# Down-projection as seven streamed products instead of full products in six groups of inner tiles

## The chip, the cores and the metric

One core of a Trainium2 chip runs the kernel. The metric is the device time of one execution in microseconds (us). TensorE (PE) multiplies, VectorE (DVE), ScalarE (ACT) and GpSimd (POOL) do the elementwise work, and SyncE (SP) issues most transfers. Each engine works its own queue in order; semaphores hold an instruction until what it needs is there.

## The reference

One layer for 1024 tokens of width 1024, in fp32: a token mixer and its output projection, a layer norm over a scaled residual, a gated MLP with a causal convolution, and a second layer norm. The change lies in the last product of the MLP.

```python
def layer_norm(x, g, b):
    ...
    y = (xf - mu) * lax.rsqrt(var + LN_EPS)
    return (y * g + b).astype(x.dtype)

def conv_gated_mlp(h, w_up, conv_w, conv_b, w_down):
    u = jnp.einsum('btd,df->btf', h, w_up)
    ...
    uc = conv_b + sum(conv_w[j] * up[:, j:j + T] for j in range(CONV_WIDTH))
    a, v = jnp.split(uc, 2, axis=-1)
    return jnp.einsum('btf,fd->btd', jax.nn.gelu(a) * v, w_down)
    ...
    h = layer_norm(ALPHA * h + mix, ln1_g[l], ln1_b[l])
    ffn = conv_gated_mlp(h, w_up[l], conv_w[l], conv_b[l], w_down[l])
    h = layer_norm(ALPHA * h + ffn, ln2_g[l], ln2_b[l])
```

T = 1024 tokens, D = 1024, 2816 inner channels, which are 22 tiles of 128 (`f` = 0 to 21).

## The kernel before

**Products.** An fp32 operand is split into a high part (`split`, L69, a copy to fp32r on ACT) and a low part (L70, a subtraction on DVE). `mm3` (L86 to L89) makes a product of three matmuls: high by high, high by low, low by high. One matmul has a 128x128 stationary tile and 512 columns. A `unit` is a PSUM tile of 128x1024, two banks.

**Up-projection.** It is a form of Strassen's scheme already. `prep(f)` loads the two weight tiles of f and makes seven combinations on DVE; `pair(f)` runs seven products, 84 matmuls, and puts them together in `ua` and `uv` (L688, L691, L694 on DVE); `post(f)` is the convolution of both (L698 on ACT, L700 on DVE), the GELU (L710, ACT), the product of the gate (L712, DVE) and one store of the gated tile to DRAM, `gd[f]` (L713, 512 KB). They are generators; `step` runs the pieces of pair(f), post(f-1) and prep(f+1) in turn, and this order, with the tile scheduler's, sets the queues.

**Down-projection.** The 22 inner tiles come in groups of 2, 4, 4, 4, 4, 4 (`GRP`). For a group, each of the 8 token tiles t and both column halves are multiplied over the inner tiles of the group in PSUM: 22 x 8 x 2 x 3 = 1056 matmuls. DVE then adds the unit to `z[t]` in SBUF (L811 in the first group, with the shift of the residual; L813 in the others). For the next group, `down_weight(f)` and `gated(f)` load a tile of w_down and one of `gd` through SP into `raw` (three buffers) and split them: weights into `wh`/`wl` or `dh`/`dl`, gated tiles into the eight places of `bh` and `bl`. `residual()` loads `zn` from `zd[t]` (L788) and adds it, scaled, to z[t] (L789, L790 on DVE).

**Layer norm.** In the last group z[t] is drained (L801), its statistics are taken (L500, L471), `rs` is made on GpSimd (L463, L464), and z is scaled. Tiles 1, 3, 5 and 6 do it "spread": L476 on DVE, L477 on ACT, the addition of beta on GpSimd (L480), a store through SP (L481). The others use two operations on DVE (L491, L495) and L497; the last tile in halves.

Of the kernel before, what the change touches and what calls it, by code (L numbers as in the profile page):

```python
# [27 lines left out]
GRP = (2,) + (4,) * 5  # L28
# [9 lines left out]
SPLIT = 5  # L38
SPREAD = (1, 3, 5, 6)
# [6 lines left out]
def block_kernel(ctx: ExitStack, tc: tile.TileContext, x, xT, w_ct, w_i, pool_w, w_out, w_up, w_down, pk, rows, masks, ident, out):  # L46
# [7 lines left out]
    big = ctx.enter_context(tc.tile_pool(name="big", bufs=1))  # L54
# [646 lines left out]

    def post(f):
        a, v = outs.pop(f)
        cv, ca = (ug.tile([P, T], F32, tag=f"c{n}", name=f"c{n}") for n in "va")
# [8 lines left out]
        nc.sync.dma_start(out=gd[f], in_=ca)  # L713
# [49 lines left out]
    def first_group():
        for f in groups[0]:
            down_weight(f)
            yield
        for i in range(3):
            yield
        for f in groups[0]:
            gated(f)  # L770
            yield
# [118 lines left out]
```

## Time and profile before

| | us |
|---|---|
| median of three runs | 1072.68 (1071.88 to 1073.37) |
| the profiled execution | 1071.9 |
| its span | 1070.0 |
| PE busy | 1055.3 (99%), 4812 matmuls |
| DVE busy | 767.2 (72%) |
| ACT busy | 402.6 (38%) |
| GpSimd busy | 50.9 (5%) |
| end of the up-projection's last matmul | 820.4 |
| end of the last matmul | 1060.8 |

Busy time is counted per engine; matmuls are pipelined, so the distance from start to start is the cost of one. A number in square brackets behind a row is the time that the engine was idle before it, with the operation that released it.

### The profile page before, as it was taken

To read this page: it belongs to the slowest core of one execution; us is meant where nothing else is said; L and a number is where in the kernel's file an instruction comes from. 1 tells how busy PE (TensorE), PEld (TensorE's weight loads), DVE (VectorE), ACT (ScalarE), POOL (GpSimd) and SP (SyncE) were. 2 spreads that over 40 slices of the span, in tenths; PEclk is the share of its full clock that TensorE was granted. 3 is DMA by queue.
4 is the path that set the end of the run, shared out by engine and by line. 5 is a ranking of instruction groups with operands and counts; after the bars stand their busy time and mean duration, and the time that the engine had idled before them with its cause. 6 is when DMAs were issued, how large, how long until landed. Compare 5 with 4: busy or idle time off the path is not lost.

```text
span 1070.0 us, 11956 instructions
## 1 busy us (share of the span) xinstructions
PE 1055.3 (99%) x4812; PEld 861.5 (81%) x4812; DVE 767.2 (72%) x891; ACT 402.6 (38%) x500; POOL 50.9 (5%) x71
## 2 busy tenths in 40 slices
PE   8999999999999999999999999999999999999996
PEld 6888888888888877887777778778777888888885
DVE  6585498877736689877868868778778965634178
ACT  5422453223713474544434444445355312202001
POOL 2000000011000100000000000000000000000035
PEclk9999999999999999999999999999999999999999
DMA  8200211100142313231231221322326644321012
GB/s 319 90 20 1 79 40 40 40 1 20 41 177 99 122 75 118 79 118 60 72 106 59 89 89 59 112 65 62 116 79 216 236 138 157 119 97 59 1 60 99
DMA packets 27848, 97.13 MB, mean 91 GB/s; under 512 B 3088, under 2 KB 3984, under 8 KB 27792
## 3 DMA queue, kind: packets, MB, share of 16 engines
q1 hardware_dynamic: 27648, 96.29, 26.3%
q8 instruction: 38, 0.62, 0.2%
q14 instruction: 18, 0.15, 0.0%
q10 hardware_dynamic: 144, 0.07, 0.0%
HBM read 76.42 MB, written 19.92 MB: 90 GB/s over the span
## 4 chain that ended last, share of the span: by engine, by line
PE 89%; DVE 4%; POOL 2%; ACT 2%; DMA 2%; issue 1%; SPq 0%; POOLq 0%; DVEq 0%; ACTq 0%
PE u L87 28%; PE u L89 28%; PE u L88 28%; PE u L230 3%; POOL rs L463 1%; POOL z L480 1%; PE u L270 1%; PE u L272 1%; PE u L259 1%; DMA hg<-in_xT 1%; ACT hq L533 1%; DVE st L500 1%; DVE wl L70 1%; DMA raw<-gd 0%; DVE bl L70 0%
## 5 line engine op out<-in xcount | busy, mean ns | idle before, releaser
L87 PE MATMUL u<-bh,wh 128*128 128x512 f32 x520 | 206.2, 398 | 2.9 <-DVE uv L691 1.3
L88 PE MATMUL u<-bl,wh 128*128 128x512 f32 x520 | 203.0, 390 | 1.0 <-DVE bl L70 1.0
L89 PE MATMUL u<-bh,wl 128*128 128x512 f32 x520 | 203.0, 391 | 0.0
L69 ACT ACTIVATE wh<-raw 128x1024 fp32r<-128x1024 f32 x97 | 100.7, 1058 | 133.2 <-PE u L88 100.8
L70 DVE TENSOR_TENSOR wl<-raw,wh 128x1024 fp32r<-128x1024 f32 x97 | 116.8, 1223 | 28.1 <-ACT wh L69 25.7
L87 PE MATMUL u<-wh,bh 128*128 128x512 f32 x336 | 132.6, 395 | 0.0
L89 PE MATMUL u<-wh,bl 128*128 128x512 f32 x336 | 131.1, 390 | 0.0
L88 PE MATMUL u<-wl,bh 128*128 128x512 f32 x336 | 131.0, 390 | 0.0
L87 PEld LDWEIGHTS u<-bh,wh 128*128 128x128 f32 x520 | 97.7, 188 | 30.3 <-DVE uv L691 7.7
L88 PEld LDWEIGHTS u<-bl,wh 128*128 128x128 f32 x520 | 97.7, 188 | 20.8 <-DVE bl L70 1.6
L89 PEld LDWEIGHTS u<-bh,wl 128*128 128x128 f32 x520 | 97.6, 188 | 20.7
L87 PE MATMUL u<-th,wh 128*128 128x512 f32 x264 | 105.5, 400 | 0.0
L89 PE MATMUL u<-th,wl 128*128 128x512 f32 x264 | 103.6, 393 | 0.5 <-DVE wl L70 0.5
L88 PE MATMUL u<-tlo,wh 128*128 128x512 f32 x264 | 103.1, 391 | 0.0
L813 DVE TENSOR_TENSOR z<-u,z 128x1024 f32<-128x1024 f32 x32 | 39.1, 1223 | 62.2 <-PE u L89 62.2
L89 PEld LDWEIGHTS u<-wh,bl 128*128 128x128 f32 x336 | 63.1, 188 | 13.5
L88 PEld LDWEIGHTS u<-wl,bh 128*128 128x128 f32 x336 | 63.2, 188 | 13.1
L87 PEld LDWEIGHTS u<-wh,bh 128*128 128x128 f32 x336 | 63.1, 188 | 13.1
L87 PEld LDWEIGHTS u<-th,wh 128*128 128x128 f32 x264 | 49.5, 187 | 18.4 <-DVE uv L688 4.3
L88 PE MATMUL u<-dl,bh 128*128 128x512 f32 x160 | 63.4, 396 | 0.0
L89 PE MATMUL u<-dh,bl 128*128 128x512 f32 x160 | 63.4, 396 | 0.0
L87 PE MATMUL u<-dh,bh 128*128 128x512 f32 x160 | 63.3, 396 | 0.0
(175 smaller groups left out, 1631.8 us busy)
## 6 DMA issues: line engine op xcount, KB each, us to landing
raw<-in_w_up SPq DMA_DIRECT2D x42, 512.0 KB, 3.4
gd<-ca SPq DMA_DIRECT2D x22, 512.0 KB, 5.3
raw<-in_w_down SPq DMA_DIRECT2D x22, 512.0 KB, 4.3
raw<-gd SPq DMA_DIRECT2D x22, 512.0 KB, 4.0
raw<-in_w_ct SPq DMA_DIRECT2D x13, 512.0 KB, 3.3
raw<-in_w_out SPq DMA_DIRECT2D x8, 512.0 KB, 3.2
z<-in_x SPq DMA_DIRECT2D x8, 512.0 KB, 4.1
zd<-z SPq DMA_DIRECT2D x8, 512.0 KB, 2.6
```

Source lines behind the costliest of these rows:

```text
L69: A.activation(out=h, in_=r, func=AF.Copy)
L70: V.tensor_tensor(out=l, in0=r, in1=h.bitcast(F32), op=ALU.subtract)
L87: PE.matmul(o, lhsT=ah, rhs=bh, start=start, stop=False, **kw)
L88: PE.matmul(o, lhsT=ah, rhs=bl, start=False, stop=False, **kw)
L89: PE.matmul(o, lhsT=al, rhs=bh, start=False, stop=stop, **kw)
L230: PE.matmul(ul[:, p * P:(p + 1) * P], lhsT=km[:, p * P:(p + 1) * P], rhs=view(QF, p * P + hh, [2 * hh, 64 // hh], [512 - hh, 2], [1, hh]), ...
L259: PE.matmul(up[:, c * P:(c + 1) * P], lhsT=KTr[:, c * P:(c + 1) * P], rhs=vchunk(c, hs), start=True, stop=True)
L270: PE.matmul(uo[:, cs], lhsT=vchunk(c, hs), rhs=sc[:, cs], start=True, stop=c == 0)
L272: PE.matmul(uo[:, cs], lhsT=S[:, (c - 1) * P:c * P], rhs=QF[:, cs], start=False, stop=True)
L463: G.tensor_scalar(out=rs, in0=mv[:, 1:2], scalar1=LN_EPS, scalar2=None, op0=ALU.add)
L480: G.tensor_tensor(out=zt[:, c], in0=zt[:, c], in1=bet[:, c], op=ALU.add)
L813: V.tensor_tensor(out=z[t], in0=u, in1=z[t], op=ALU.add)
```

## The change

**Products.** The down-projection becomes seven products of halves: token halves (`lo`, `hi` of 512), even and odd inner tiles, column halves. Each has 11 pairs of inner tiles, 4 token tiles and 512 columns: 7 x 11 x 4 x 3 = 924 matmuls. They run as seven rounds over all inner channels in the order P1, P2, P6, P5, P7, P3, P4. A round has six steps (`jps`): five of two pairs, 24 matmuls, and one of a single pair, 12.

**PSUM.** A round's four token tiles keep four banks for the whole inner sum. P1, P6, P7 and P4 use one set, P2, P5 and P3 the other; P6, P7 and P3 go on from the sum that stands there. `finish` (L877, L880) adds a bank to z once per round.

**Gated side.** `post` stores seven kinds of 128x512 blocks (`gd["11"]` to `gd["s4"]`) per pair of f, 2 KB to a row, and makes the four combinations on DVE (L718, L720, L723, L725). For each step SP loads the two blocks (`load_a`, L769).

**Weights.** Blocks of w_down are loaded by 24 transfers through GpSimd's queue (`load_w2`, L852) into `ww`, in memory that the up-projection's operands held; only two for P1 go through SP into `rawb` (L797). Combinations are made on DVE in `prepare` (L806, L811, L818, L820), and each operand is split one step ahead (L65 on ACT, L66 on DVE).

**Layer norm.** Tiles 0 to 5 are "added": L472 on DVE, L473 on ACT, then a transfer from GpSimd's queue that adds the row of beta to z (L474), then the store (L475). Tile 6 is "whole", tile 7 in halves on DVE. In P4 token tiles 0 and 1 run together through all steps, then 2, then 3.

```diff
-GRP = (2,) + (4,) * 5
...
+    jps = [(j, j + 1) if j + 1 < NF // 2 else (j,) for j in range(0, NF // 2, 2)]
+    gd = {(n, i): tc.dram_tile([P, len(js), 512], F32, name=f"gd{n}{i}")
+          for n in ("11", "12", "22", "s1", "s2", "s3", "s4") for i, js in enumerate(jps)}
...
-        if how == "spread":
+        if how == "added":
             V.scalar_tensor_tensor(out=zt, in0=zt, scalar=mv[:, 0:1], in1=gam, op0=ALU.subtract, op1=ALU.mult)
             A.activation(out=zt, in_=zt, func=AF.Identity, scale=rs)
-            def shift(c):
-                G.tensor_tensor(out=zt[:, c], in0=zt[:, c], in1=bet[:, c], op=ALU.add)
-                nc.sync.dma_start(out=sink[:, c], in_=zt[:, c])
-            if last:
-                shift(halves[0])
-                late_shift.append(lambda: shift(halves[1]))
-            else:
-                shift(whole)
+            G.dma_start(out=zt, in_=rows[3:4, :].broadcast_to([P, D]), accum_op=ALU.add)
+            nc.sync.dma_start(out=sink, in_=zt)
...
+    def store(n, j, src):
+        nc.sync.dma_start(out=gd[n, j // 2][:, j % 2, :], in_=src)
...
-        nc.sync.dma_start(out=gd[f], in_=ca)
+        j = f // 2
+        if f % 2 == 0:
+            gated[j] = ca
+            store("11", j, ca[:, lo])
+            return
+        store("12", j, ca[:, lo])
+        store("22", j, ca[:, hi])
+        yield
+        g1 = gated.pop(j)
+        sm = ug.tile([P, T], F32, tag="cv", name="sm")
+        V.tensor_tensor(out=sm[:, lo], in0=g1[:, lo], in1=g1[:, hi], op=ALU.add)
+        store("s3", j, sm[:, lo])
+        V.tensor_tensor(out=g1[:, hi], in0=g1[:, hi], in1=ca[:, hi], op=ALU.add)
+        store("s1", j, g1[:, hi])
+        yield
+        V.tensor_tensor(out=sm[:, hi], in0=g1[:, hi], in1=g1[:, lo], op=ALU.add)
+        store("s2", j, sm[:, hi])
+        V.tensor_tensor(out=g1[:, lo], in0=sm[:, hi], in1=ca[:, lo], op=ALU.add)
+        store("s4", j, g1[:, lo])
...
-    wd = [None] * NF
-    def down_weight(f):
-        if f % 10 < 5:
-            wd[f] = weight(w_down[f])
-            return
-        r = raw(w_down[f])
-        wd[f] = [dn.tile([P, 1024], F32R, tag=f"d{n}", name=f"d{n}") for n in "hl"]
-        split(r, *wd[f])
-    def gated(f):
-        r = raw(gd[f])
-        split(r, bh[:, f % 8, :], bl[:, f % 8, :])
...
+    order = ("11", "12", "s2", "s1", "s3", "s4", "22")
+    P1, P2, P6, P5, P7, P3, P4 = range(7)
+    plan = [(i, q) for i in range(7) for q in range(NS)]
+    raw_a, opsd = {}, {}
+    def load_a(n):
+        i, q = plan[n]
+        r = raw_a[n] = rawp.tile([P, 2, 512], F32, tag="raw", name="rawa")
+        nc.sync.dma_start(out=r[:, :len(jps[q]), :], in_=gd[order[i], q])
...
+    def slot(n):
+        if n >= 2 * NS * P4 and n - 2 * NS * P4 < 4:
+            t = zq.tile([P, 4, 512], F32R, tag=f"w0{n - 2 * NS * P4}", name="p4")
+            return t[:, 0:2], t[:, 2:4]
+        if n % 8 < 5:
+            return [t.rearrange("p (a t) -> p a t", t=512) for t in wpair()]
+        return [dn.tile([P, 2, 512], F32R, tag=f"d{e}", name=f"d{e}") for e in "hl"]
...
+    def prepare(n):
+        i, q = plan[n]
+        k = len(jps[q])
+        a = split2(raw_a.pop(n)[:, :k, :], 2 * n, k)
+        if i == P1 and q < 2:
+            src = rawp.tile([P, 2, 512], F32, tag="raw", name="rawb")[:, :k]
+            nc.sync.dma_start(out=src, in_=w_view(0, q, lo))
+        elif i == P1:
+            src = w_block(0, q, lo)
+        elif i == P2:
+            src = w_block(1, q, lo)
+            w11 = w_block(0, q, lo)
+        elif i == P6:
+            w21, w22 = w_block(1, q, lo), w_block(1, q, hi)
+            src = zq.tile([P, 2, 512], F32, tag="t2", name="t2")[:, :k]
+            V.scalar_tensor_tensor(out=src, in0=w_block(0, q, lo), scalar=-1.0, in1=w22, op0=ALU.mult, op1=ALU.subtract)
+        elif i == P5:
+            src = w_block(0, q, lo)
+        elif i == P7:
+            src = w_block(0, q, hi)
+            V.tensor_tensor(out=src, in0=w_block(1, q, hi), in1=src, op=ALU.subtract)
+        elif i == P3:
+            src = w_block(1, q, hi)
+        else:
+            src = w_block(1, q, lo)
+        opsd[n] = a, split2(src, 2 * n + 1, k)
+        if i == P2:
+            V.tensor_tensor(out=w11, in0=w11, in1=w_block(0, q, hi), op=ALU.subtract)
+        elif i == P6:
+            V.tensor_tensor(out=w21, in0=w21, in1=src, op=ALU.add)
...
+    step([pair(NF - 1), post(NF - 2), first_operands()], 7)
+    last_post = post(NF - 1)
+    step([last_post], 7)
...
+    w_loads = [(0, q, lo) for q in range(2, NS)] + [(1, q, lo) for q in range(NS)] + [(0, q, lo) for q in range(2)] + \
+              [(0, q, hi) for q in range(NS)] + [(1, q, hi) for q in range(NS)]
+    def load_w2(n):
+        for r_, q, c in w_loads[:n]:
+            G.dma_start(out=w_block(r_, q, c), in_=w_view(r_, q, c))
+        del w_loads[:n]
...
-            for u, c in zip(us, halves):
-                for f in fs:
-                    mm3(u[:, c], bh[:, f % 8, ts], bl[:, f % 8, ts], wd[f][0][:, c], wd[f][1][:, c], f == fs[0], f == fs[-1])
-                if last and t >= SPLIT:
-                    drain(u, c)
-            if not last:
-                if gi == 0:
-                    V.scalar_tensor_tensor(out=z[t], in0=b1_, scalar=ALPHA, in1=u, op0=ALU.mult, op1=ALU.add)
-                else:
-                    V.tensor_tensor(out=z[t], in0=u, in1=z[t], op=ALU.add)
-                if ahead:
-                    f = ahead.pop(0)
-                    down_weight(f)
-                    gated(f)
-                elif left and gi:
...
+    cs = [unit() for i in range(2)]
+    banks = {1: [cs[p // 2][:, halves[p % 2]] for p in range(4)]}
+    fresh = {P1: 1, P2: 3, P5: 3, P4: 1}
+    where = {P1: 1, P6: 1, P7: 1, P4: 1, P2: 3, P5: 3, P3: 3}
...
+    def multiply(n, ps_):
+        i, q = plan[n]
+        (ah, al), (wh, wl) = opsd[n]
+        for p in ps_:
+            o = banks[where[i]][p]
+            for jj in range(len(jps[q])):
+                ts = slice(p * P, (p + 1) * P)
+                mm3(o, ah[:, jj, ts], al[:, jj, ts], wh[:, jj], wl[:, jj], i in fresh and q == 0 and jj == 0,
+                    q == NS - 1 and jj == len(jps[q]) - 1, skip_group_check=True)
...
+    def advance(n):
+        nonlocal prepared
+        while prepared <= n and prepared < len(plan):
+            if prepared not in raw_a:
+                load_a(prepared)
+            prepare(prepared)
+            prepared += 1
+            if prepared < len(plan) and prepared not in raw_a:
+                load_a(prepared)
+            load_w2(2)
+    for n in range(6 * NS):
+        i, q = plan[n]
+        if n == NS:
+            cs += [unit() for e in range(2)]
+            banks[3] = [cs[2 + p // 2][:, halves[p % 2]] for p in range(4)]
+        advance(n + 1)
+        multiply(n, range(4))
+        if q == NS - 1:
+            for p in range(4):
+                finish(i, p)
+            if i == P6:
+                beside += [lambda t=t: (residual(t), stats(z[t], lo, st6[:, t])) for t in range(4)]
+            elif i == P7:
+                beside += [lambda t=t: (residual(t), stats(z[t], hi, st6[:, t])) for t in range(4, 8)]
+        elif beside:
+            beside.pop(0)()
+            if i == P3 and not beside:
+                g2, b2 = row(2, "g"), row(3, "b")
+    n0 = 6 * NS
+    for q in range(NS):
+        advance(n0 + q + 1)
+        multiply(n0 + q, (0, 1))
+        if q < 4:
+            norm2(q, hi, "added")
+    for p in range(2):
+        finish(P4, p)
+    for q in range(NS):
+        multiply(n0 + q, (2,))
+    for p in range(2):
+        norm2(4 + p, lo, "added")
+    finish(P4, 2)
+    for q in range(NS):
+        multiply(n0 + q, (3,))
+    norm2(6, lo, "whole")
+    finish(P4, 3)
+    norm2(7, lo, "halves")
```

DVE at the end of the up-projection, first before, from the last addition to `ca` in `conv` (L700): `z` is a result tile, `row` a parameter row, `zn` the residual, `dl` the low part of a weight tile.

```order
L700 SCALAR_TENSOR_TENSOR ca<-ua,pkt,ca 128x1022 [waits DVE_49]
L811 SCALAR_TENSOR_TENSOR z_5703<-row_5711,u 128x1024 [waits PE_49]
L70 TENSOR_TENSOR bl<-raw,bh 128x1024 [waits DMAHW0_49]
L712 TENSOR_TENSOR ca<-ca,cv 128x1024 [waits Activation_49]
L811 SCALAR_TENSOR_TENSOR z_5704<-row_5711,u 128x1024 [waits PE_49]
L70 TENSOR_TENSOR bl<-raw,bh 128x1024 [waits DMAHW4_49]
L811 SCALAR_TENSOR_TENSOR z_5705<-row_5711,u 128x1024 [waits PE_49]
L811 SCALAR_TENSOR_TENSOR z_5706<-row_5711,u 128x1024 [waits PE_49]
L789 SCALAR_TENSOR_TENSOR zn<-zn,row_5709 128x1024 [waits DMAHW1_49]
L70 TENSOR_TENSOR dl<-raw,dh 128x1024 [waits DMAHW3_49,Activation_49]
```

The same place after the change: L687 is `conv`, L707 the product of the gate, w_5828 the weight block of the third step of P1.

```order
L687 SCALAR_TENSOR_TENSOR ca<-ua,pkt,ca 128x1022 [waits DVE_49]
L707 TENSOR_TENSOR ca<-ca,cv 128x1024 [waits Activation_49]
L720 TENSOR_TENSOR ca<-ca 128x512 [waits DVE_49]
L723 TENSOR_TENSOR sm<-ca 128x512 [waits DVE_49]
L725 TENSOR_TENSOR ca<-sm,ca 128x512 [waits DMAHW6_49,DVE_49]
L858 SCALAR_TENSOR_TENSOR zn<-zn,row_5846 128x1024 [waits DMAHW7_49,DMAHW1_49,DMAHW0_49]
L66 TENSOR_TENSOR dl<-w_5828,dh 128x1024 [waits DMASW0_49,Activation_49]
L66 TENSOR_TENSOR dl<-rawa,dh 128x1024 [waits DMAHW5_49,Activation_49]
```

Behind the product of the gate there now stand three additions, then the residual's first operation, which waits for its load, and behind it the low parts of the third step.

SP there, before: `gd_2012` and `gd_2013` are the last two gated tiles, `zd` the residual's tiles.

```order
L713 DMA gd_2012<-ca 128x1024 [waits DVE_49]
L65 DMA raw<-in_w_down 128x1024 [waits DMAHW3_49,DVE_49]
L65 DMA raw<-gd_1996 128x1024 [waits DMAHW5_49,DMAHW0_49,DVE_49]
L788 DMA zn<-zd_1984 128x1024 [waits PE_49]
L788 DMA zn<-zd_1985 128x1024
L65 DMA raw<-in_w_down 128x1024 [waits DMAHW4_49,DVE_49]
L65 DMA raw<-gd_1997 128x1024 [waits DMAHW7_49,DVE_49]
L65 DMA raw<-in_w_down 128x1024 [waits DMAHW0_49,DVE_49]
L713 DMA gd_2013<-ca 128x1024 [waits DMAHW6_49,DVE_49]
```

And after, where L694 is `store` and L857 the load of the residual.

```order
L769 DMA rawa<-gd_1998 128x1024 [waits DMAHW0_49,DVE_49]
L694 DMA gd_2003<-ca 128x512 [waits DVE_49]
L694 DMA gd_2009<-ca 128x512
L694 DMA gds_2015<-ca 128x512 [waits DMAHW5_49,DVE_49]
L694 DMA gds_2021<-sm 128x512 [waits DVE_49]
L694 DMA gds_2033<-ca 128x512 [waits DMAHW7_49,DVE_49]
L857 DMA zn<-zd_1984 128x1024
L857 DMA zn<-zd_1985 128x1024 [waits DMAHW4_49,DMAHW3_49,DMAHW1_49]
L769 DMA rawa<-gd_1999 128x1024 [waits DMAHW2_49,DVE_49]
```

The loads of `zn` stood ahead of the last gated store; they now stand behind the five stores of the last pair.

GpSimd's queue at the same place, after the change (before it holds only the `rs` and beta operations of the layer norm from here on):

```order
L464 TENSOR_TENSOR rs<-rs,epst 128x1 [waits Pool_49]
L852 DMA w_5828<-in_w_down 128x2x512 [waits DVE_49,PE_49,Activation_49]
L852 DMA w_5829<-in_w_down 128x2x512
L852 DMA w_5830<-in_w_down 128x2x512
L852 DMA w_5831<-in_w_down 128x512
L852 DMA w_5832<-in_w_down 128x2x512
L852 DMA w_5833<-in_w_down 128x2x512
L852 DMA w_5834<-in_w_down 128x2x512 [waits DMAHW0_49,DVE_49]
```

The loads of w_down stand on GpSimd one behind the other. The first waits for the last matmuls of the up-projection, whose operands lie in that memory.

## Rows read from the trace of the kernel before

**Rows 1.** Page, parts 1 and 2: busy PE, and its clock in 40 slices.

```profile
PE 1055.3 (99%) x4812; PEld 861.5 (81%) x4812; DVE 767.2 (72%) x891; ACT 402.6 (38%) x500; POOL 50.9 (5%) x71
...
PEclk9999999999999999999999999999999999999999
```

**Rows 2.** Windows (columns in the order PE, PEld, DVE, ACT, POOL, PEclk, DMA, GB/s).

```profile
410.00:800.00 390.00, 389.55 (x1677) 309.86 (x1676) 309.04 (x345) 178.33 (x205) 0.00 (x0) 1.00 0.26 82
820.40:1060.80 240.40, 240.40 (x1043) 195.65 (x1042) 147.11 (x144) 43.74 (x42) 19.84 (x17) 1.00 0.32 110
```

**Rows 3.** Timeline of PE (start, us, engine, line), end of the up-projection.

```profile
817.38 0.50 PE L87 MATMUL u<-bh,wh 128*128 128x512 f32 x1 [1.30 <-DVE uv L691]
```

**Rows 4.** Timeline of DVE, from the end of the up-projection.

```profile
815.49 1.23 DVE L70 TENSOR_TENSOR bl<-raw,bh 128x1024 fp32r<-128x1024 f32 x1 [3.45 <-ACT bh L69]
...
820.70 0.69 DVE L694 TENSOR_TENSOR ua<-u,ua 128x512 f32<-128x512 f32 x1
821.30 1.27 DVE L700 SCALAR_TENSOR_TENSOR cv<-uv,pkt,cv 128x1022 f32<-128x1022 f32 x1
822.49 1.22 DVE L70 TENSOR_TENSOR wl<-raw,wh 128x1024 fp32r<-128x1024 f32 x1
823.62 1.28 DVE L700 SCALAR_TENSOR_TENSOR ca<-ua,pkt,ca 128x1023 f32<-128x1023 f32 x1
...
835.07 1.22 DVE L789 SCALAR_TENSOR_TENSOR zn<-zn,row 128x1024 f32<-128x1024 f32 x1
836.21 1.22 DVE L70 TENSOR_TENSOR dl<-raw,dh 128x1024 fp32r<-128x1024 f32 x1
```

**Rows 5.** Timeline of ACT there, the last GELU.

```profile
828.11 1.04 ACT L710 ACTIVATE ca<-ca 128x1024 f32<-128x1024 f32 x1
```

**Rows 6.** Timeline of SP's queue there.

```profile
817.12 0.90 SPq L788 DMA_DIRECT2D zn<-zd  x2
...
830.65 0.32 SPq L713 DMA_DIRECT2D gd<-ca  x1
```

**Rows 7.** View of the tile zn, its transfers.

```profile
DMA to landing us min/median/max: 3.2/4.2/7.0
```

**Rows 8.** Window of the busiest transfers, start of the kernel.

```profile
8.00:10.00 2.00, 2.00 (x10) 1.45 (x8) 1.09 (x1) 1.66 (x2) 0.00 (x0) 1.00 1.03 415
```

**Rows 9.** Windows after the last matmul.

```profile
1065.00:1066.00 1.00, 0.00 (x0) 0.00 (x0) 0.60 (x1) 0.00 (x0) 0.37 (x1) 0.86 0.29 111
1066.00:1067.00 1.00, 0.00 (x0) 0.00 (x0) 0.95 (x3) 0.00 (x0) 0.00 (x0) 0.50 0.00 0
```

**Rows 10.** Timeline of PE, start of the kernel.

```profile
1.04 3.43 PE L336 MATMUL u<-warm 128*128 128x256 bf16 x16 [1.04 <-DVE epst L383]
```

**Rows 11.** Waits of DVE, 430 to 790 (us in total, times, longest).

```profile
DVE uv L691 <- PE u L89: 55.2, 19, 3.1
```

**Rows 12.** Timeline of DVE at the end.

```profile
1056.98 2.27 DVE L476 SCALAR_TENSOR_TENSOR z<-z,mv,row 128x1024 f32<-128x1024 f32 x1
...
1062.31 0.21 DVE L471 BATCH_NORM_AGGREGATE mv<-st 128x2 f32<-128x12 f32 x1
...
1065.40 1.54 DVE L495 SCALAR_TENSOR_TENSOR z<-z,rs,row 128x512 f32<-128x512 f32 x3 [0.46 <-POOL rs L464]
```

**Rows 13.** Timeline of POOL at the end.

```profile
1052.57 1.30 POOL L463 TENSOR_SCALAR rs<-mv 128x1 f32<-128x1 f32 x1 [2.98 <-DVE mv L471]
1053.96 0.56 POOL L464 TENSOR_TENSOR rs<-rs,epst 128x1 f32<-128x1 f32 x1
...
1061.25 2.48 POOL L480 TENSOR_TENSOR z<-z,row 128x512 f32<-128x512 f32 x2 [1.26 <-ACT z L477]
```

**Rows 14.** Page, part 6: transfers (size, median us to landing).

```profile
raw<-in_w_down SPq DMA_DIRECT2D x22, 512.0 KB, 4.3
...
raw<-in_w_i SPq DMA_DIRECT2D x4, 512.0 KB, 5.5
row<-in_rows SPq DMA_DIRECT2D x4, 512.0 KB, 4.0
```

More of the change, by code (lines that the diff above doesn't have):

```diff
@@ L763, in first_group @@
[L763 to L775 removed]
+    NS = len(jps)
+    order = ("11", "12", "s2", "s1", "s3", "s4", "22")
+    P1, P2, P6, P5, P7, P3, P4 = range(7)
+    plan = [(i, q) for i in range(7) for q in range(NS)]
@@ L790, in residual @@
         V.tensor_tensor(out=z[t], in0=z[t], in1=zn, op=ALU.add)
-    for gi, fs in enumerate(groups):
-        last = gi == len(groups) - 1
-        ahead = [] if last else list(groups[gi + 1])
-        for t in range(NC):
-            ts = slice(t * P, (t + 1) * P)
-            st6 = small.tile([P, 2, 6], F32, tag="st6", name="st6") if last else None
-            us = [unit(), unit()] if last and t >= SPLIT else [unit()] * 2
-            def drain(u, c):
-                V.tensor_tensor(out=z[t][:, c], in0=u[:, c], in1=z[t][:, c], op=ALU.add)
-                stats(z[t], c, st6)
-            for u, c in zip(us, halves):
-                for f in fs:
-                    mm3(u[:, c], bh[:, f % 8, ts], bl[:, f % 8, ts], wd[f][0][:, c], wd[f][1][:, c], f == fs[0], f == fs[-1])
-                if last and t >= SPLIT:
-                    drain(u, c)
-            if not last:
-                if gi == 0:
-                    V.scalar_tensor_tensor(out=z[t], in0=b1_, scalar=ALPHA, in1=u, op0=ALU.mult, op1=ALU.add)
-                else:
-                    V.tensor_tensor(out=z[t], in0=u, in1=z[t], op=ALU.add)
-                if ahead:
-                    f = ahead.pop(0)
-                    down_weight(f)
-                    gated(f)
-                elif left and gi:
-                    residual()
-                    if not left:
-                        g2, b2 = row(2, "g"), row(3, "b")
-                continue
-            if t < SPLIT:
-                for c in halves:
-                    drain(u, c)
-            layer_norm(z[t], g2, b2, st6, "spread" if t in SPREAD else "whole" if t < NC - 1 else "halves", out[t * P:(t + 1) * P, :], t == NC - 2)
@@ new lines, in first_touch, with more, finish @@
+    def first_touch(t, c, src, op):
+        V.scalar_tensor_tensor(out=z[t][:, c], in0=b1_[:, c], scalar=ALPHA, in1=src, op0=ALU.mult, op1=op)
+    def more(t, c, src, op):
+        V.tensor_tensor(out=z[t][:, c], in0=z[t][:, c], in1=src, op=op)
+    def finish(i, p):
+        c = banks[where[i]][p]
+        if i == P1:
+            first_touch(p, lo, c, ALU.add)
+        elif i == P2:
+            more(p, lo, c, ALU.add)
+        elif i == P6:
+            first_touch(p, hi, c, ALU.add)
+        elif i == P5:
+            first_touch(4 + p, hi, c, ALU.subtract)
+        elif i == P7:
+            more(4 + p, hi, c, ALU.subtract)
+            first_touch(4 + p, lo, c, ALU.subtract)
+        elif i == P3:
+            more(p, hi, c, ALU.add)
+        else:
+            more(4 + p, lo, c, ALU.add)
```

60 lines of the change are left out of this document (38 added, 22 removed).

## Prediction

> **What bounds the kernel now.** I read the shares of the page first. TensorE (PE) is busy 1055.3 of the 1070.0 us span, and its granted clock shows nine tenths or more in every slice [rows 1]. So the time is the number of matmuls times their pitch, plus the few places where PE stands. The window over the down-projection alone says the same: 240.40 us, all busy, at clock 1.00 [rows 2]. Of its 1056 matmuls (22 inner tiles x 8 token tiles x 2 column halves x 3) some stand in that window beside a few of the up-projection; the trace holds 1043 there, so one costs 240.40 / 1043 = 0.2305 us. VectorE (DVE) is busy 147.11 of the 240.40 us there, 309.04 of 390.00 us in the up-projection: beside PE, not on the path.
>
> The profiled execution took 1071.9 us, the median of the three is 1072.68. I make the sum against 1071.9 and add 0.8 at the end.
>
> **What goes.** Seven products of 11 inner pairs x 4 token tiles x 3 matmuls are 924, where there were 1056: 132 fewer of the same form, each with its own weight load. PE's weight loader is busy 195.65 of 240.40 us in the window [rows 2], so the new order, which has one load per matmul as before, cannot make it the bound. 132 x 0.2305 = **-30.4 us**, all of it on the path.
>
> The one stall of PE before the end of the up-projection goes too: 1.30 us at 817.38 for `uv` [rows 3]. Ahead of `uv` on DVE stood `bl`, which waited 3.45 us for ScalarE's `bh` [rows 4], the split of a gated tile just stored and loaded again. In the changed order no split of a freshly loaded tile stands ahead of `uv` in the last pair. **-1.3 us.**
>
> **What comes at the seam.** Let t0 be the end of the last up-projection matmul (820.4 before). The changed order of PE has 38 matmuls behind t0 (12 of the first step, 24 of the second, 2 of the third) until one needs `dl`, the low part of w02: 38 x 0.2305 = 8.8 us of work. DVE works its queue in order, and ahead of that `dl` stand, from the same operations before and the spacing of their starts [rows 4]: `ua` at t0+0.30, 0.60; `cv` 1.19; a `wl` 1.13; `ca` as `cv`; a `wl`; `ca` again: done at t0+6.73. The GELU on ScalarE takes 1.04 [rows 5], so the product of the gate starts at 7.8 and ends at 8.95; three half-width additions, 0.60 each, end at 10.75. Then stands L858, `zn<-zn,row`, the residual of a token tile that is added to z only after the third round, and it waits for its load. That load stands on SP's queue behind the five stores of the last gated pair, the last of which waits for the third addition. So it is issued at about t0+11.0. In the kernel before it was issued at 817.12, ahead of the last gated store at 830.65 [rows 6], and still DVE came to it only at 835.07 [rows 4]. From issue to landing such a load takes 3.2, 4.2 or 7.0 us (least, median, most) [rows 7]. It would land at t0+14.2, 15.2 or 18.0; two operations of 1.14 (`zn`, `dl`) put PE's operand at t0+16.5, 17.5 or 20.3. PE stands for 7.7, 8.7 or 11.5 us.
>
> I take the last. Five stores of 256 KB stand before the 512 KB load on its queue, of them 0.75 MB issued in the last 2 us, while GpSimd's queue, free since t0, brings in 512 KB blocks of w_down without pause. The transfers reach 415 GB/s at a share of 1.03 [rows 8]; with half of that, 1.25 MB take 6 us. That is nearest to the 7.0, for which **+11.5 us** stands; with ends 7.7 and 14 (a third of the rate instead of a half, 9 us).
>
> A stall of that length costs the clock too. After the last matmul of before (1060.8, the end of the window in [rows 2]) the granted clock was still 0.86 from 1065 to 1066 and 0.50, the lower level of 1.2 GHz, after it [rows 9]. On coming back, the matmuls run at the lower level for a time. The start of the kernel gives a size: 16 matmuls of 256 columns took 3.43 us, 214 ns each [rows 10], double what the pitch of 0.2305 for 512 columns makes (115 ns). The same stretch at half speed loses **+1.7 us** (0 if the stall is short, 3.4 if it lasts twice as long).
>
> **What comes elsewhere.** In the up-projection, DVE gets four half-width additions per pair of f, 0.60 each [rows 4]: 2.4 us per 39 us, in which DVE is busy 79% and waits for PE up to 3.1 us in each f ahead of `uv` [rows 2, 11]. They fit; where they push a `uv` late PE waits for it. **+0.5** (0 to 3). Stores in rows of 2 KB, seven halves instead of four per pair of f, add 75% to the bytes stored, at a DMA share of 0.26: nothing.
>
> In the rounds, operands of step n+1 are split in step n: at most two loads, four splits of 1.22 and a combination in 5.5 us of PE (24 x 0.2305), less on average: DVE about three quarters busy. Drains into z happen once per round into the other bank set, which has a whole round (30.4 us) for it. Nothing. In the last round the layer-norm operations of z0 to z3 stand ahead of the last splits of DVE; adding durations of the same operations, the last one is ready 15.5 us after the round before, where PE has 64 x 0.2305 = 14.8 us of work: **+0.7** (0 to 2, since an L476 took 2.27 beside GpSimd's L480 [rows 12]; none stands beside it now).
>
> **The tail.** Before, the chain after the last matmul was 9.2 us. `rs` on GpSimd could start at 1063.7 only, because L480 held that engine from 1061.25 for 2.48 us, though `mv` was there at 1062.52, and L495 started with it at 1065.40 [rows 12, 13]. Without tensor work on GpSimd, `rs` takes 1.30 + 0.09 + 0.56 [rows 13], which puts L495 at 1064.5: **-0.9 us**. The additions of beta by DMA for z4 and z5 are issued some 8 and 7 us before the last matmul ends; SP's stores of z7 stand behind the stores that wait for them, so they cost only if they take over 12 us; no row shows such a transfer, the nearest is the load of a row of the same size, 4.0 us [rows 14]. Nothing (0 to 3).
>
> **Sum.** -30.4 - 1.3 + 11.5 + 1.7 + 0.5 + 0.7 - 0.9 = -18.2; 1071.9 - 18.2 = 1053.7, with 0.8 about **1055 us**. The ends of the unknown terms (stall 7.7 to 14, clock 0 to 3.4, up-projection 0 to 3, last round 0 to 2, tail 0 to 3) make 1048 to 1064.
>
> **Rivals.** *No stall at the seam.* If the residual's load lands before DVE reaches it, -30.4 - 1.3 + 1.2 - 0.9 = -31.4, about 1041; up to 1046 with a short one. The order of both queues speaks against it: only the price of the load is free, not its place. 0.10.
>
> *The weight loads are the bound (the slower side).* All of w_down but two blocks now comes through GpSimd's queue, 24 loads that start at t0 (nothing else stands on that queue until the `rs` of the last round), and no transfer of that queue is in this trace. If they land one after another, P us apart, the first to be late are the 14th, which DVE needs about 6.5 us before the third step of the second round (t0 + 50, so P above 3.1), and the 19th, needed 7 us before the third round (t0 + 62, P above 3.3). Each further microsecond of P costs 19. At the full rate P is 0.512 MB / 415 GB/s = 1.26 us [rows 8], and nothing is late. At 4.3, the median of a w_down load on SP's queue taken from issue to landing and one after another [rows 14], 19 x 4.3 = 82 against 62: +20, about 1074; at 5.5 (the `in_w_i` loads [rows 14]) 1097. The gain is eaten at P = 4.2. SP's queue issued two such loads within 0.9 us [rows 6], though one takes over 3: queued loads overlap, which speaks for the low price. For a high one speaks that GpSimd and DVE hinder each other: an operation of DVE took 2.27 us beside GpSimd's L480, 1.22 for the like of it (L789) alone [rows 4, 12]. The Trainium skill, page "SBUF — State Buffer", section "SBUF: two separate sides", says that descriptors of a DMA issued from GpSimd are written by that engine, that DVE in a two-port fast mode locks it out, and that such a DMA should go to the queue of SP or ScalarE; by that rule the loads wait for DVE, and this rival holds. The trace shows the conflict of two engines but no such load, and the same section ties the lock to fast modes, while DVE's work here runs at 1.2 ns an element [rows 4]. Slower 0.08, level with before 0.03, in between (1060 to 1070) 0.07.
>
> *The up-projection stretches.* If each pair of f lost 0.5 to 1 us to the additions, +5 to +10: 1060 to 1065. The 55.2 us that DVE waited ahead of `uv` in 19 f [rows 11] speak against. 0.07.
>
> **Chances.** Forecast (1048 to 1060) 0.65, no or short stall 0.10, loads 0.18, stretched up-projection 0.07. Faster by over 0.2% (about what a measurement of this kernel can tell): 0.65 + 0.10 + 0.07 + 0.07 = 0.89; within it 0.03; slower 0.08. The range 1046 to 1066 leaves out the slow and level loads (0.11) and most of the stall-free case (0.08).
>
> **What the changed profile would show.** 924 L83 to L85 matmuls of the down-projection 0.23 us apart; one idle of PE of 8 to 14 us some 9 us after the last up-projection matmul, put down to DVE `dl`, behind an idle of DVE before L858 that ends with the landing of `zn`; the clock below full there and back a few us later; no other idle of PE above 1 us. Wrong would be an idle of PE that follows a GpSimd-queue load, idles spread over the up-projection, or no idle at the seam.

## The result and the profile after

| | before | after |
|---|---|---|
| median of four runs, us | 1072.66 (1071.88 to 1073.37) | 1059.22 (1058.49 to 1060.02) |
| ratio to before | | 0.9875 (95%: 0.9858 to 0.9892) |
| profiled execution; its span | 1071.9; 1070.0 | 1058.64; 1056.6 |
| PE busy; idle in the span | 1055.3; 14.7 | 1026.0; 30.6 |
| last up-projection matmul ends | 820.4 | 817.5 |
| last matmul ends; from there to the end | 1060.8; 9.2 | 1046.9; 9.7 |

The kernel is 13.4 us faster, 1.25%. I forecast 1055 in a range of 1046 to 1066. The page of after, parts 1 and 2, against [rows 1]:

```profile
PE 1026.0 (97%) x4680; PEld 839.2 (79%) x4680; DVE 812.4 (77%) x973; ACT 437.8 (41%) x542; POOL 62.0 (6%) x96
...
PEclk9999999999999999999999999999999799999998
DMA  8200211100142223224214323322233982352448
```

PE has 132 matmuls fewer and 29.3 us less to do, but stands 15.9 us longer in the span, and the row of the clock now has a dip just where the DMA row has its peak. The waits of PE in after (columns: us in total, times, longest) say where it stands:

```profile
PE u L84 <- DVE dl L66: 15.3, 1, 15.3
...
PE u L83 <- DVE z L880: 0.8, 1, 0.8
...
PE u L83 <- ACT dh L65: 0.6, 1, 0.6
```

One wait of 15.3 us is over half of all the idle time. It lies at the seam, for `dl`, as forecast. The timeline of DVE there (start, us, what; in brackets the idle time before it), to be read beside [rows 4]:

```profile
828.18 0.69 DVE L725 TENSOR_TENSOR ca<-sm,ca 128x512 f32<-128x512 f32 x1
840.10 1.22 DVE L858 SCALAR_TENSOR_TENSOR zn<-zn,row 128x1024 f32<-128x1024 f32 x1 [11.23 <-DMA zn<-zd]
841.24 1.22 DVE L66 TENSOR_TENSOR dl<-w,dh 128x1024 fp32r<-128x1024 f32 x1
```

And SP's queue, beside [rows 6]:

```profile
829.38 0.32 SPq L694 DMA_DIRECT2D gds<-ca  x1
829.76 5.18 SPq L857 DMA_DIRECT2D zn<-zd  x2
```

The third addition (828.18) is followed by the residual's operation, which idles 11.23 us for its load; `dl` comes behind it. The load was issued at 829.76, behind the last store, and landed 10.3 us later, which is the largest in the view of the tile `zn` (least, median, most; [rows 7] before):

```profile
DMA to landing us min/median/max: 3.1/4.4/10.3
```

Windows over the seam (columns as in [rows 2]):

```profile
830.00:832.00 2.00, 0.00 (x0) 0.00 (x0) 0.00 (x0) 0.26 (x1) 0.72 (x1) 0.66 1.02 399
...
846.00:848.00 2.00, 2.00 (x7) 1.51 (x6) 2.00 (x3) 0.00 (x0) 0.76 (x2) 0.58 0.94 313
848.00:850.00 2.00, 2.00 (x10) 1.63 (x9) 0.20 (x1) 0.00 (x0) 0.00 (x0) 1.00 0.99 369
```

And the window of the first 12 matmuls after the stall:

```profile
842.50:847.60 5.10, 5.09 (x12) 4.03 (x13) 5.10 (x6) 0.00 (x0) 2.41 (x4) 0.50 0.97 333
```

The transfers ran at full rate (share 0.94 to 1.02 in these rows, 313 to 399 GB/s) through the stall and past it. The granted clock fell from 1.00 to 0.50 and stayed there for 5 us after work came back at 842.5: 12 matmuls took 5.1 us at the lower level, where 12 at the pitch of 0.2305 take 2.8.

### The profile page after: what moved, and what is told of

Its sections match the earlier page's. It is cut to its first block, busy times and chain, and to the rows that moved or that the text cites. A ratio compares the mean times of both kernels' runs of the same rounds, so it can differ in the third digit from the quotient of the medians.

```text
span 1056.6 us, 12003 instructions
## 1 busy us (share of the span) xinstructions
PE 1026.0 (97%) x4680; PEld 839.2 (79%) x4680; DVE 812.4 (77%) x973; ACT 437.8 (41%) x542; POOL 62.0 (6%) x96
## 4 chain that ended last, share of the span: by engine, by line
PE 92%; DVE 3%; DMA 3%; ACT 2%; issue 0%; SPq 0%; POOL 0%; POOLq 0%; DVEq 0%; ACTq 0%
PE u L83 29%; PE u L85 29%; PE u L84 29%; PE u L228 3%; DMA zn<-zd 1%; DMA gd<-ca 1%; PE u L268 1%; PE u L270 1%; PE u L257 1%; DMA hg<-in_xT 1%; ACT hq L520 1%; DMA raw<-in_w_up 1%; DVE wl L66 1%; ACT fh L520 0%; PE u L529 0%
## 5 line engine op out<-in xcount | busy, mean ns | idle before, releaser
L65 ACT ACTIVATE wh<-raw 128x1024 fp32r<-128x1024 f32 x85 | 88.6, 1057 | 113.1 <-PE u L84 81.3
L66 DVE TENSOR_TENSOR wl<-raw,wh 128x1024 fp32r<-128x1024 f32 x85 | 103.0, 1225 | 25.7 <-ACT wh L65 23.2
L65 ACT ACTIVATE wh<-rawa 128x1024 fp32r<-128x1024 f32 (+1 forms) x30 | 30.1, 1002 | 91.6 <-PE u L84 74.9
L85 PEld LDWEIGHTS u<-th,wl 128*128 128x128 f32 x264 | 49.6, 188 | 12.3 <-DVE wl L66 1.2
L83 PE MATMUL u<-wh,bh 128*128 128x512 f32 x144 | 57.8, 401 | 0.0
L84 PEld LDWEIGHTS u<-tlo,wh 128*128 128x128 f32 x264 | 49.6, 188 | 9.7
L687 DVE SCALAR_TENSOR_TENSOR cv<-uv,pkt,cv 128x1023 f32<-128x1023 f32 (+1 forms) x44 | 56.1, 1276 | 0.3 <-ACT cv L685 0.2
L85 PE MATMUL u<-wh,wl 128*128 128x512 f32 x144 | 56.2, 391 | 0.0
L84 PE MATMUL u<-wl,wh 128*128 128x512 f32 x144 | 56.2, 390 | 0.0
L85 PE MATMUL u<-wh,bl 128*128 128x512 f32 x144 | 56.2, 390 | 0.0
L687 DVE SCALAR_TENSOR_TENSOR ca<-ua,pkt,ca 128x1023 f32<-128x1023 f32 (+1 forms) x44 | 56.1, 1276 | 0.0
L83 PE MATMUL u<-wh 128*128 128x512 f32 x144 | 56.1, 390 | 0.0
```

The source lines that it names most:

```text
L65: A.activation(out=h, in_=r, func=AF.Copy)
L66: V.tensor_tensor(out=l, in0=r, in1=h.bitcast(F32), op=ALU.subtract)
L83: PE.matmul(o, lhsT=ah, rhs=bh, start=start, stop=False, **kw)
L84: PE.matmul(o, lhsT=ah, rhs=bl, start=False, stop=False, **kw)
L85: PE.matmul(o, lhsT=al, rhs=bh, start=False, stop=stop, **kw)
L687: V.scalar_tensor_tensor(out=c[:, 2 - j:], in0=u[:, :T - 2 + j], scalar=pkt[:, cw + j:cw + j + 1], in1=c[:, 2 - j:], op0=ALU.mult, op1=ALU ...
```

## Experiments

Each ran beside the kernel before on the same chip; ratios are to it.

**The residual later.** The residual's tiles take the places of `t2`, which the third round uses; loads and operation leave the seam.

```diff
-            src = zq.tile([P, 2, 512], F32, tag="t2", name="t2")[:, :k]
+            src = zq.tile([P, 2, 512], F32, tag="t2", name="t2", bufs=2)[:, :k]
...
-        zn = zq.tile([P, D], F32, tag="zn", name="zn", bufs=2)
+        zn = zq.tile([P, D], F32, tag="t2", name="zn", bufs=2)
```

> The residual's tiles take the places of the combination t2, so that its loads and its first operation move from the seam to the third and fourth round; nothing else changes. Theory (the 15.3 us stall of TensorE is the in-order wait of VectorE for the residual's load): the low part dl starts right after the third addition at about t0 + 11.3, the stall falls to about 3 us, the clock stays at its upper level, and the time falls by 12.3 + 2.3 to about 1044.5 us. Rival (the weight block through GpSimd's queue, or ScalarE's dh, would have been as late): the stall stays above 10 us and the time above 1053.

Measured: 1045.82 us (1044.45 to 1047.10), ratio 0.9751 (0.9736 to 0.9765). DVE at the seam:

```profile
829.36 0.69 DVE L725 TENSOR_TENSOR ca<-sm,ca 128x512 f32<-128x512 f32 x1
829.96 1.22 DVE L66 TENSOR_TENSOR dl<-w,dh 128x1024 fp32r<-128x1024 f32 x1
```

PE there:

```profile
827.61 0.74 PE L83 MATMUL u<-dh,wh 128*128 128x512 f32 x2 [0.57 <-ACT dh L65]
831.24 0.50 PE L84 MATMUL u<-dl,wh 128*128 128x512 f32 x1 [2.89 <-DVE dl L66]
```

Windows there, columns as in [rows 2]:

```profile
830.00:832.00 2.00, 0.76 (x3) 0.67 (x4) 2.00 (x3) 1.43 (x3) 0.10 (x1) 1.00 1.01 392
832.00:834.00 2.00, 2.00 (x7) 1.54 (x6) 2.00 (x3) 0.00 (x0) 1.00 (x2) 0.59 1.05 417
834.00:836.00 2.00, 2.00 (x7) 1.59 (x6) 1.79 (x3) 0.00 (x0) 0.91 (x2) 0.56 1.03 397
```

`dl` follows the third addition at once, the stall is 2.89 us, and 13.4 us are gone. The wait for the load was the cause; the weight block was there. One thing I had wrong: I expected the clock to stay up after so short a stall. The window in which PE came back shows 1.00, the two after it 0.59 and 0.56. The price stands in PE's timeline:

```profile
832.28 0.56 PE L85 MATMUL u<-dh,wl 128*128 128x512 f32 x1
...
835.92 0.39 PE L83 MATMUL u<-dh,wh 128*128 128x512 f32 x1
```

Nine matmuls start from 832.28 to 835.92 and take 3.6 us, 2.1 at the pitch: 1.6 us lost. The four executions of this kernel took 1044.45 us at a mean granted clock of 0.998, 1045.30 (the profiled one) at 0.995, 1046.34 and 1047.10 at 0.993. The longer ones had the lower clock, so what such a stall costs beside its length seems to change from execution to execution; the trace is of one only.

**The load alone.** The residual's first load is kept behind the five stores; GpSimd copies one column of it into the place of the fifth weight block, so that this block and all behind it wait for the landing. The load's use on DVE falls behind the splits.

```diff
+    early[0] = zq.tile([P, D], F32, tag="zn", name="zn", bufs=2)
+    nc.sync.dma_start(out=early[0], in_=zd[0])
+    G.tensor_copy(out=w_block(1, 0, lo)[:, 0, 0:1], in_=early[0][:, 0:1])
```

> The residual's first load keeps its place behind the five stores, its use by VectorE falls behind the splits, and GpSimd's queue holds the fifth and later weight blocks until that load has landed. It measures the load alone. Theory A (the load took 10.3 us because the weight blocks shared the transfer rate): issue to landing 3 to 5 us. Theory B (the five stores ahead on its own queue delay it): 8 to 11 us, as before. The time lies near that of the run with the residual late in either case, 1043 to 1048 us, if the weights, which start some 15 us later, are not late.

Measured, one run: 1047.91 us. SP's queue:

```profile
829.23 0.40 SPq L694 DMA_DIRECT2D gds<-ca  x1
832.44 0.32 SPq L914 DMA_DIRECT2D zn<-zd  x1
```

GpSimd's:

```profile
835.79 0.19 POOL L915 COPY w<-zn 128x1 f32<-128x1 f32 x1 [14.51 <-DMA zn<-zd]
```

The load was issued at 832.44 and released the copy 3.3 us later, at 835.75; with the weight blocks beside it, it had taken 10.3. But it was issued 3.2 us after the last store and not 0.4, since in this order it waits until stores have landed (2.7 us among SP's waits). So from the last store's issue to the landing it is 6.5 us here, 10.7 in after: at least 4.2 us come from the weight blocks, up to 3.2 from the stores ahead, the rest is the load. Both theories hold a part; the first the larger one.

**The weight blocks on SP's queue.** On top of the late residual.

```diff
-            G.dma_start(out=w_block(r_, q, c), in_=w_view(r_, q, c))
+            nc.sync.dma_start(out=w_block(r_, q, c), in_=w_view(r_, q, c))
```

> As the run with the late residual, with the 24 weight blocks on SP's queue. Theory (GpSimd's queue is not what limits the loads): no gain from SP; since the blocks now stand behind the five stores of the last pair, they start at about t0 + 11 instead of t0 + 1 and the first is late: a stall of 7 to 9 us at the seam, about 1050 to 1054 us. Rival (the issue from GpSimd, locked out by VectorE, slows each block): single blocks land in 3 to 4 us instead of 6, and the time is below that of the run with the late residual.

Measured, one run: 1052.48 us. PE at the seam:

```profile
835.89 1.22 PE L83 MATMUL u<-dh,wh 128*128 128x512 f32 x2 [9.60 <-ACT dh L65]
```

The transfers of the weight blocks (KB each, median us to landing):

```profile
w<-in_w_down SPq DMA_DIRECT2D x20, 512.0 KB, 9.2
```

The same in after:

```profile
w<-in_w_down POOLq DMA_DIRECT2D x20, 512.0 KB, 6.0
```

The blocks start behind the stores, and PE waits 9.6 us for the first. Through SP a block takes longer, 9.2 us, not the 3 to 4 of the rival. Fourteen are queued there at once, so the likely reason is that they share the transfer rate; that is argued, not shown. GpSimd's queue is the better place here.

**The splits before the additions.** On top of the late residual: the third weight block comes through SP, and `prepare(1)` and `prepare(2)` are emitted between the product of the gate and the additions. (The list of loads through GpSimd is reordered to match, and eight of its 24 are issued at the start instead of four.)

```diff
     last_post = post(NF - 1)
-    step([last_post], 7)
+    step([last_post], 5)
+    uap.__exit__(None, None, None)
+    dn = ctx.enter_context(tc.tile_pool(name="dn", bufs=3, side="right", reuse_waits="tile"))
+    prepare(1)
+    load_a(2)
+    prepare(2)
+    load_a(3)
+    step([last_post], 2)
...
-        if i == P1 and q < 2:
+        if i == P1 and q < 3:
```

> On top of the late residual: the weight block of the third step comes through SP ahead of the seam, and its split and that of the fourth step's gated block are emitted between the product of the gate and the three additions of the last pair, which move behind them one by one. Theory (what is left of the stall is the additions in VectorE's in-order queue, and the fall of the clock follows from the stall's length): dl starts right behind the gate's product, the stall falls from 2.9 to about 1 us, the clock stays up, the time falls by 2 + 1.7 to about 1042 us. Rival (ScalarE's dh or the gated block is as late as the additions were; the clock falls all the same): time above 1044.

Measured: 1041.13 us (1040.88 to 1041.48), ratio 0.9711 (0.9698 to 0.9724). DVE at the seam:

```profile
826.31 1.22 DVE L66 TENSOR_TENSOR dl<-rawb,dh 128x1024 fp32r<-128x1024 f32 x1
827.45 0.69 DVE L720 TENSOR_TENSOR ca<-ca 128x512 f32<-128x512 f32 x1
```

PE there:

```profile
827.59 0.51 PE L84 MATMUL u<-dl,wh 128*128 128x512 f32 x1 [0.54 <-DVE dl L66]
```

The window behind it:

```profile
830.00:832.00 2.00, 2.00 (x10) 1.59 (x9) 2.00 (x3) 1.81 (x2) 1.16 (x3) 1.00 1.00 364
```

The stall is 0.54 us and the clock stays at 1.00. The time fell by 4.7 us (4.4 between the profiled executions) where the two idles at the seam (2.89 and 0.57) shrank to 0.54, by 2.9. The rest, 1.8 us (1.5), is what the fall of the clock had cost; it agrees with the 1.6 read from the timeline above.

**The stores by ScalarE's queue.** On the changed kernel.

```diff
-            nc.sync.dma_start(out=sink, in_=zt)
+            nc.scalar.dma_start(out=sink, in_=zt)
```

> Stores of the six tiles whose beta is added by a transfer go through ScalarE's queue, so that the stores of tiles 6 and 7 do not stand behind them on SP. Theory (the tail of 9.7 us holds a wait on SP for the addition to tile 5): tile 6 leaves some 7 us earlier, the last store is issued some 1.4 us earlier, the tail is 8.3 us and the time 1057.8. Rival (the transfers themselves are slow beside the additions, whichever queue they stand on): tail 9.2 to 9.7, time within 0.5 of 1059.2.

Measured: 1058.90 us (1056.85 to 1060.16), ratio 0.9867 (0.9850 to 0.9883), no difference from after. ScalarE at the end:

```profile
1029.59 2.83 ACTq L475 DMA_DIRECT2D out<-z  x2
1032.52 2.19 ACT L473 ACTIVATE z<-z,rs 128x1024 f32<-128x1024 f32 x2 [6.98 <-DMA z<-in_rows]
```

DVE there:

```profile
1046.62 1.28 DVE L483 SCALAR_TENSOR_TENSOR z<-z,rs,row 128x1024 f32<-128x1024 f32 x1 [4.47 <-POOL rs L464]
```

This tells nothing on the theory. ScalarE works in order too: its store of the first tile waits for that tile's addition, and the norm operations of tiles 2 to 5 (L473) wait behind it, so that the later additions start later and tile 6 waits 4.47 us for its `rs` on GpSimd. The queue's wait was only moved.

**Tiles 4 and 5 on VectorE.** On top of the late residual.

```diff
-        norm2(4 + p, lo, "added")
+        norm2(4 + p, lo, "whole")
```

> On top of the late residual: tiles 4 and 5 are normed by two operations on VectorE, as tile 6 is, instead of the addition by transfer; no such addition is under way in the last 10 us. Theory (the stores of the last tiles stood on SP behind those that wait for the additions of tiles 4 and 5, and beside their traffic): the time from the last matmul to the end falls from 9.7 to about 8.3 us, the time to about 1044.4. Rival (VectorE's two extra operations of 1.28 us push the last drain): 9.5 us or more, time 1045.8 or above.

Measured: 1046.91 us (1046.02 to 1048.94), ratio 0.9767 (0.9754 to 0.9780). PE in the last round:

```profile
1027.92 0.50 PE L83 MATMUL u<-p,p 128*128 128x512 f32 x1 [2.56 <-DVE z L880]
```

DVE there:

```profile
1025.98 1.28 DVE L483 SCALAR_TENSOR_TENSOR z<-z,rs,row 128x1024 f32<-128x1024 f32 x1 [0.46 <-POOL rs L464]
1027.19 0.68 DVE L880 TENSOR_TENSOR z<-z,u 128x512 f32<-128x512 f32 x1
```

The tail is 8.2 us (1037.4 to 1045.6), as the theory says. But PE waits 2.56 us for the drain of the third token tile, which now stands behind the norms on DVE: both halves of the question were right, and the second costs more than the first gives. PE waits at all only because the last token tile uses the other half of the same PSUM tile. The wait costs more than its length, since the clock fell again:

```profile
1028.00:1030.00 2.00, 2.00 (x6) 1.59 (x7) 1.93 (x3) 0.00 (x0) 1.07 (x1) 0.58 0.94 379
1030.00:1032.00 2.00, 2.00 (x7) 1.59 (x6) 1.23 (x2) 0.00 (x0) 0.81 (x2) 0.57 1.00 393
```

**All together,** and the last token tile of P4 in a bank of the other set:

```diff
+            o = banks[3][0] if (i, p) == (P4, 3) else banks[where[i]][p]
```

> The late residual, the splits before the additions, tiles 4 and 5 normed on VectorE, and the last token tile of P4 in a bank of the other set, so that its matmuls do not wait 0.8 us for the drain of the tile before it. If the three are independent, 1045.8 - 3.7 - 1.4 - 0.8 = about 1040 us. If they share a cover (the additions pushed behind the splits make the stores of the last pair late), 1042 to 1044.

Measured: 1039.13 us (1037.93 to 1039.58), ratio 0.9691 (0.9677 to 0.9704). PE's waits:

```profile
PE u L85 <- DVE wl L66: 1.2, 1, 1.2
...
PE u L84 <- DVE dl L66: 0.5, 1, 0.5
```

The wait for the drain is gone, the one at the seam is 0.5 (the one of 1.2 lies at 412.9, at the start of the up-projection), and the tail is 8.2 us (1028.6 to 1036.8). The edits add up, to 1039 where 1040 was expected, and this version beats both kernels.

**Without the additions,** to price them, on top of the version before. The same blocks are stored with other numbers in them, so what this kernel computes is not the layer.

```diff
-        V.tensor_tensor(out=sm[:, lo], in0=g1[:, lo], in1=g1[:, hi], op=ALU.add)
...
-        V.tensor_tensor(out=g1[:, lo], in0=sm[:, hi], in1=ca[:, lo], op=ALU.add)
```

> As the run with all edits, but the four additions that make s1 to s4 are left out for all eleven pairs; the same number and size of blocks is stored, with operands that are there, so the rounds P6, P5, P7 and P3 multiply other numbers. It prices the additions. Theory (they fit beside TensorE in the up-projection): the span from 430 to 800 us holds as many matmuls, within 1 in 400, and the time is 0 to 1 us below 1039.1, most of it at the seam, where two additions stand between splits. Rival (VectorE's extra work stretches the up-projection a little in every f): 2 to 5 us below.

Measured: 1038.87 us (1038.81 to 1039.29), ratio 0.9690 (0.9674 to 0.9706), no difference from the version before. A window of the up-projection without the additions:

```profile
440.00:798.00 358.00, 358.00 (x1544) 285.19 (x1543) 280.30 (x313) 160.23 (x185) 0.00 (x0) 1.00 0.32 105
```

In after:

```profile
440.00:798.00 358.00, 358.00 (x1548) 286.88 (x1546) 303.10 (x353) 160.84 (x185) 0.00 (x0) 1.00 0.31 105
```

Before:

```profile
440.00:798.00 358.00, 358.00 (x1541) 284.74 (x1540) 279.79 (x312) 160.70 (x185) 0.00 (x0) 1.00 0.26 83
```

DVE is 23 us less busy without them, and PE gets nothing for it. The version with all edits, which differs by the additions alone, shows the same as after: 1547 matmuls, DVE busy 303.37. They were free.

**Operands of a step from one pool.** On top of the late residual.

```diff
-        if n % 8 < 5:
+        if (n % 8 < 5) if n >= 2 * NS * P4 else (n // 2 % 3 < 2):
```

> On top of the late residual: the operand places are handed out so that both operands of a step come from the same pool (two steps from wp, one from dn), except in the last round. In the changed kernel matmuls with both operands in one pool started 0.227 to 0.230 us apart, those of a dn operand with a wp operand 0.233 to 0.234. Theory (the pairing of places sets the pitch): the mixed steps of the first six rounds vanish, all matmuls there start 0.227 to 0.230 apart, about 1.2 us less in all. Rival (the pitch goes with what else runs): some dn steps still show 0.233.

Measured, one run: 1046.11 us. Groups by form between 850 and 1008 (xcount, busy, mean ns) in after:

```profile
L84 PE MATMUL u<-wl,wh 128*128 128x512 f32 x116 | 45.3, 390 | 0.0
...
L84 PE MATMUL u<-dl,wh 128*128 128x512 f32 x59 | 23.4, 396 | 0.0
```

The same in this kernel:

```profile
L84 PE MATMUL u<-wl,wh 128*128 128x512 f32 x160 | 62.5, 391 | 1.4 <-DVE wl L66 1.4
...
L84 PE MATMUL u<-dl,dh 128*128 128x512 f32 x62 | 24.3, 392 | 0.0
```

The mixed group, 396 ns, is gone there, and what is left is at 389 to 393. The gain did not show: the kernel got a new wait of 1.4 us for `wl` (in the row above), and 1.2 us is at the edge of what one run can tell. Inconclusive for the time.

## Why the prediction was right, and where its sizes were off

The mechanism and its place were right: the saving of PE's work is real, and half of it goes to one stall at the seam, behind a residual load that nobody needs there.

- *Fewer matmuls, -30.4.* The count is 4680 for 4812, 132 fewer. From 817.5 to 1046.9 the 912 matmuls behind the seam's start took 229.4 us; without the stalls (15.3, 0.6, 0.8) and with the 12 slow ones taken out, 900 in 207.6 us, 0.2307 each: the pitch of [rows 2].
- *The stall for `uv`, -1.3.* Gone: no such row among PE's waits.
- *The seam, +11.5.* Mis-sized. The working had the load issued at t0 + 11.0, landing 7.0 later, and `dl` ready at t0 + 20.3. With t0 = 817.5 it was issued at t0 + 12.2 (the third addition ended at 11.3 for 10.75), took 10.3, and `dl` was ready at t0 + 24.8. PE stood 15.3 us, with 0.6 for `dh` before. The end that I gave for a third of the transfer rate was 14. I had taken half, as if the queues shared the rate evenly; the run with the weights held shows that 4.2 us came from the blocks of GpSimd's queue, and that the stores ahead hold a further part.
- *The clock, +1.7.* Measured 2.3 in after (5.1 us for 12 matmuls, 2.8 at the pitch), 1.6 in the run with the residual late. That it lasts some 3.6 us after a stall of 3.5, about as long as I took from the kernel's start, was not foreseen: I had put 0 for a short one. The row that I sized it by does not show the lower level itself: the windows of before give 1.00 from 0 to 5 us, and only the 214 ns of a matmul pointed to it.
- *The up-projection, +0.5.* Wrong sign: it ends 2.9 us earlier, of which 1.3 is the stall above; 1.6 is gained. The window of 358 us holds 1548 matmul records for 1541. The additions do not cost anything, as the run without them shows; why the pitch is 0.4% lower is open. Without the additions the window holds 1544, in all other runs of this section 1546 to 1548, so the lower pitch is no accident of one execution. How much of it arrives at the seam varies: in the other runs with the additions the up-projection's last matmul ends up to 1.6 us later than here.
- *The last round, +0.7.* The size came out (0.8) by luck, the cause did not: no split was late. PE waited for a drain, since two token tiles share a PSUM tile, which I had not looked at.
- *The tail, -0.9.* Wrong: +0.5. `rs` came earlier as worked out (L483 starts 3.6 us after the last matmul, L495 had started 4.6 after), but the stores were late. I had let the additions by transfer cost nothing unless they took over 12 us. They took up to 10.6, and that was enough: tile 5's store waited on SP for its addition, and tile 6's, ready 7 us before, came out behind it and beside those of tile 7.

The additions by transfer in after (least, median, most):

```profile
DMA to landing us min/median/max: 5.0/7.3/10.6
```

SP's queue at the end of after:

```profile
1028.24 22.24 SPq L475 DMA_DIRECT2D out<-z  x6
1050.57 3.19 SPq L484 DMA_DIRECT2D out<-z  x4
```

The six stores take 22 us of SP's queue, the first of tiles 6 and 7 goes out at 1050.57, and four issues take 3.19 us. The run with tiles 4 and 5 on VectorE takes this away: 8.2 us.

The measured terms give -30.4 - 1.3 + 15.9 + 2.3 - 1.6 + 0.8 + 0.5 = -13.8, against 13.3 between the profiled executions; 0.5 is not assigned. The working gave -18.2. Of the 4.9 us between, the seam is 4.4, the clock 0.6, the tail 1.4, the up-projection -2.1. So there is some luck in the number: the seam lies outside the ends that I gave it (15.9 against 7.7 to 14), and the up-projection, out the other way, took back a third of what seam, clock and tail were out by. Without that the time would be near 1061, in the range still. The ends of the terms, added up again, make 1048 to 1065.5; I had written 1064.

*The rivals.* No stall: the run with the splits before the additions, where 0.54 us of the stall is left, shows what it is worth: 1041.13, the 1041 that I gave it. The weight loads as the bound: they did not come one after another. GpSimd's queue in after:

```profile
830.84 0.72 POOL L852 DMA_DIRECT2D w<-in_w_down  x1 [2.79 <-DMA rawa<-gd]
...
839.38 0.72 POOL L852 DMA_DIRECT2D w<-in_w_down  x1 [3.19 <-issue]
842.01 0.73 POOL L852 DMA_DIRECT2D w<-in_w_down  x1 [1.91 <-issue]
...
846.61 0.72 POOL L852 DMA_DIRECT2D w<-in_w_down  x1 [0.57 <-issue]
```

24 blocks went out between 818 and 862, 1.8 us apart on average, under the 3.1 from which they would be late. While DVE idled (829 to 840) five went out, and while it worked without a break (840 to 848) four in 8; an issue takes 0.72 us in both. What sets the gaps between issues, up to 3.19 us that the trace puts down to no wait, is open. The Trainium skill, "SBUF — State Buffer", section "SBUF: two separate sides", says that VectorE in a two-port fast mode keeps GpSimd from writing descriptors; no row here shows GpSimd held by VectorE in that way, and its remedy, the queue of SP, made this kernel slower for another reason (1052.48 us for 1045.82, the blocks behind the stores). A stretched up-projection did not come either: it ended earlier.

## What to carry to other kernels

Where one phase ends and another begins, read the order of each in-order queue for operations that are there only because their operands are free early: a load that is needed three rounds later cost 13.4 of 30 us because a split stood behind its first use. Price a load at such a place by the bytes that all queues have under way, not by its usual time. A stall saved is worth more than its length where the clock fell behind it: 2.9 us less of idle time gave 4.4 between the profiled executions.

## What the runs showed of the hardware that was not expected

- An idle of PE of 3.5 us (0.57 and 2.89 with two matmuls between them) was followed by 4 us at a granted clock of 0.59 and 0.56, one of 2.56 (tiles 4 and 5 on VectorE) by 4 us at 0.58 and 0.57; one of 1.37 (the run with operands from one pool) and one of 0.54 left it at 1.00. The windows show the fall after PE had come back.
- A transfer that adds 512 KB to a tile took 5.0 to 10.6 us (median 7.3), a plain load of the same row 4.3. The two were at different places in the kernel; how much of the difference is the traffic beside them is not shown.
- Matmuls with one operand in `wp` and one in `dn` last 396 ns, with both in the same pool 389 to 393; the distance of starts in the timeline differs as much, 0.234 to 0.228. In before, where `bh` lies in a third pool, it is 396 for `dl` with `bh` and 390 for `wl` with `bh`: two pools alone do not make it longer. `dn` is allocated from the right side of SBUF, `wp` and the pool of `bh` from the left; the up-projection's `w1`, also from the right, shows 394 to 396 with `bh` in after. Longer are thus the pairs with one operand on either side; whether the side is the reason is not tested.
